# First projection by chunks of tokens with two weight panels side by side, in a decoder step on one core

## The chip, the core and the metric

The kernel runs on one core of a Trainium2 chip. The core has a matrix engine (TensorE; PE in the profile, PEld its weight loads), a vector engine (VectorE, DVE), an engine for scalar functions (ScalarE, ACT), a general engine (GpSimd, POOL) and a queue that issues most transfers (SyncE, SP). The transfers themselves run on 16 DMA engines. Each engine takes its own instructions in order and waits on semaphores for the others. The metric is the device time of one launch in microseconds (us), as the median of several runs; beside it there is one profiled run, whose trace is read here.

## What is computed

One step of a decoder layer with a pooling branch and an attention branch, on 1024 prompt tokens and on 64 sample tokens (8 sequences of 8). All operands are float32. The lines that matter here are the first ones of the layer:

```python
def project(x, ln1, w_in, q_norm, k_norm):
    p = jnp.einsum('btd,de->bte', rms_norm(x, ln1), w_in)
    a, q, k, v, g_a, g_b = jnp.split(p, IN_SPLITS, axis=-1)   # 512 | 768 | 768 | 768 | 1024 | 1024
    ...
# then: a -> causal multi-scale pooling -> linear map -> w_pa; q, k, v -> dilated attention -> w_pb;
# h = x + (sigmoid(g_a) * A + sigmoid(g_b) * B) @ w_o;  y = h + relu(rmsnorm(h) @ w_up)^2 @ w_down
```

`x` has 1024 channels. `rms_norm` divides a token by the root of its mean square and multiplies by `ln1`. The kernel multiplies by `ln1` first, projects, and applies the token's factor afterwards.

## The kernel before

**Layout.** Channels lie on the 128 partitions, tokens along the free axis. 1024 channels are 8 k-tiles (`KD`). The 1088 tokens are taken in three chunks of 384, 384 and 320 columns (`CHUNKS`); the last 64 columns of the third are the sample tokens. The matmul operand `act` holds the tokens ordered by their residue modulo 4, so the split writes them with a stride.

**Two parts of a number.** Each float32 operand is split in two numbers of type fp32r, a high and a low part, and a product is the sum of three passes: high x high, high x low, low x high (`PASSES`). For x, `split_x(c, k)` does it for one k-tile of one chunk: ACT writes the high part (line 312), DVE subtracts it for the low part (line 313). For weights, `split` does the same for 512 columns of a raw panel (ACT line 116, DVE line 117).

**Weight panels.** `w_in` comes in panels of 256 output channels, 8 k-tiles wide. A panel is loaded in four quarters (`fetch`, line 127, 256 KB, two k-tiles each) into three raw buffers used in turn, and split into one of three `places`, also used in turn. The pooling input `a` (512 channels) is the first two panels, so four output tiles of 128 channels; query, key and value panels of head group 2 follow in the next places: the query panel in place 2, the key panel in place 0, the value panel in place 1.

**The first stage.** Twelve matmuls of ones run first (line 360, 24 in the trace, since a plain float32 matmul counts as two). `panel(..., first)` loads and splits panel 0; between its quarters `first(j)` loads the k-tiles 2j and 2j + 1 of chunk 0 (the first two as separate transfers of 192 KB, the others as pairs of 384 KB) and splits them. Then `pool_input(0, wt, c)` runs panel 0 over all three chunks: 48 matmuls a chunk (line 334), pair of k-tiles by pair, in each pair pass by pass, in each pass two output tiles and two k-tiles. `pool_evac` copies the two results from PSUM to `ext` on ACT (line 346; the sample columns line 351). After each chunk's matmuls come the splits of the next chunk. Panel 1 is loaded and split after that, and runs over the three chunks in the same way. There are four PSUM banks for these results, taken in turn.

**Squares.** `square_x(c)` squares the raw x of a chunk in place on ACT (line 304, held back to the matmul before it in the program by `behind_pe`), and POOL adds the four tiles to one (line 306). `x_sums(c)` sums that over the partitions with matmuls against ones (line 369, 12 in the trace) into three PSUM banks `rt`, which DVE reads (line 373). The same three banks serve all chunks. The sums of chunk 0 and 1 stand after panel 1's chunk 0 and 1, those of chunk 2 inside panel 1's chunk 2, when 36 of its 48 matmuls are done. `sample_rows` copies the sample tokens on DVE (line 284). By line 399 the norms of all three chunks are spread for the next stage, whose matmuls (lines 632, 635, 205) begin at once after the projection.

**What sets the order.** PE's order is that of the program (`manual_schedule`). On the other engines, SP's queue included, a planner fixes the order when the program is built: at each step, by its own reckoning of time, it takes from what is ready on the engine the instruction that stands first in the program. That order is then fixed, whatever the chip does; an instruction that waits holds up all behind it on its engine.

Of the kernel before, what the change touches and what calls it, by code (L numbers as in the profile page):

```python
# [15 lines left out]
P = 128  # L16
# [5 lines left out]
CH = 384  # L22
# [15 lines left out]
def decoder_step(ctx, tc, i, o):  # L38
# [10 lines left out]
    def rr(p, shape, dt, name, tag, bufs):  # L49

        n = turn[p, tag] = turn.get((p, tag), -1) + 1
        return p.tile(shape, dt, name=name, tag=f"{tag}.{n % bufs}", bufs=1)
# [38 lines left out]
    def part4(c):  # L91

        return slice(CHUNKS[c][0] // 4, (CHUNKS[c][0] + CHUNKS[c][1]) // 4)
# [12 lines left out]
    def from4(t, sub="p r l -> p l r"):  # L106
        return t.rearrange("p (r l) -> p r l", r=4).rearrange(sub)
# [7 lines left out]
    def split(dst_hi, dst_lo, src):  # L115
        ins = s_.activation(dst_hi, src, AF.Copy)  # L116
        v_.tensor_tensor(dst_lo, src, dst_hi.bitcast(F32), op=ALU.subtract)  # L117
        return ins
# [45 lines left out]
    def panel(src, name, between=None, after=None):  # L164

        n = src.shape[1]
        wt = places[:, place[0] % 3]
        place[0] += 1
        for a in range(0, n, 512):
            raw = fetch(src, name, a)  # L170
            if between is not None:
                between(a // 512)
            ins = split(wt[:, 0, a:a + 512], wt[:, 1, a:a + 512], raw)
            if after is not None:
                behind_pe(ins, after[a // 512])
        throttle.append(ins)
        return wt

    def by_k(wt, kb=KD):
        return wt.rearrange("p s (k n) -> p s k n", k=kb)  # L180
# [69 lines left out]
    def acc_tile(name, tag="acc", bufs=4):  # L250
        return rr(acc_p, [P, 512], F32, name, tag, bufs)
# [17 lines left out]
    def win(name):  # L269
        return rr(xp, [P, LS], F32, name, "win", 2)  # L270
# [10 lines left out]
    def sample_rows():  # L281
        for s in range(2):
            for k in range(KD):
                behind_pe(v_.tensor_copy(smp_t[:, k, s * NS:(s + 1) * NS].rearrange("p (l r) -> p l r", r=4),
                                         act4[s][k][:, :, SEQ // 4:].bitcast(F32).rearrange("p r l -> p l r")))
    xs = {}

    def load_x(c, j):
        c0, n = CHUNKS[c]
        x = rr(xq, [P, 2, CH], F32, name=f"xs{c}_{j}", tag="xs", bufs=12)  # L290
        if c + j == 0:

            dma(x[:, 0, :n], i["xT"][:, 0, c0:c0 + n])
            dma(cols, i["cols"])
        else:
            dma(x[:, :, :n], i["xT"][:, 2 * j:2 * j + 2, c0:c0 + n])
        xs[c, "t", j] = x[:, :, :n]
        for k in range(2):
            xs[c, 2 * j + k] = x[:, k, :n]

    def square_x(c):
        t = [xs[c, "t", j] for j in range(4)]
        for j in (3, 0, 1, 2):
            behind_pe(s_.activation(t[j], t[j], AF.Square))
        for j in range(3):
            g_.tensor_tensor(t[3], t[3], t[j], op=ALU.add)

    def split_x(c, k):
        c0, n = CHUNKS[c]
        hi, lo = (act4[s][k][:, :, part4(c)] for s in range(2))  # L310
        x = xs[c, k].rearrange("p (l r) -> p r l", r=4)
        s_.activation(hi, x, AF.Copy, scale=ln1[:, k:k + 1])  # L312
        v_.scalar_tensor_tensor(lo, x, ln1[:, k:k + 1], hi.bitcast(F32), op0=ALU.mult, op1=ALU.subtract)

    def first(j):
        if j:
            load_x(0, j)
        else:
            dma(xs[0, 1], i["xT"][:, 1, :CH])
        split_x(0, 2 * j)  # L320
        split_x(0, 2 * j + 1)

    L = 15 + SEQ
    LS = L + NB * 23
    exts = {}

    def pool_input(ja, wt, c, middle=None):
        c0, n = CHUNKS[c]
        pts = [acc_tile(f"a{2 * ja + m}_{c}") for m in range(2)]
        for k in range(0, KD, 2):  # L330
            for p, (a, b) in enumerate(PASSES):
                for m in range(2):
                    for kk in (k, k + 1):
                        last_mm[0] = t_.matmul(  # L334
                            pts[m][:, :n], wt[:, a, kk, m * P:(m + 1) * P], act4[b][kk][:, :, part4(c)],
                            start=(p == 0 and kk == 0), stop=(p == 2 and kk == KD - 1))
            if middle and k == 4:
                middle()
        return pts

    def pool_evac(ja, c, pts):
        c0, n = CHUNKS[c]
        for m in range(2):
            ext = exts[2 * ja + m]
            npr = min(n, SEQ - c0)
            s_.copy(ext[:, 15 + c0:15 + c0 + npr].rearrange("p (l r) -> p l r", r=4),
                    from4(pts[m][:, :n])[:, :npr // 4])
            if npr < n:
                new = from4(pts[m][:, :n])[:, npr // 4:].rearrange("p (t q) r -> p q r t", q=2)
                for q in range(2):  # L350
                    s_.copy(ext[:, L:].rearrange("p (b t) -> p b t", b=NB)[:, 4 * q:4 * q + 4, 15:], new[:, q])

    def open_ext(g):
        exts[g] = rr(xp, [P, LS], F32, name=f"ext{g}", tag="ext", bufs=4)
        v_.memset(exts[g][:, :15], 0.0)
# [3 lines left out]
    for _ in range(12):  # L359
        t_.matmul(wu, ones, ones, start=True, stop=True)  # L360
    load_x(0, 0)
    wt = by_k(panel(i["w_in"][0], "a0", first))
    def x_sums(c):
        n = CHUNKS[c][1]
        rt = [rr(ps, [P, 1], F32, name=f"rt{c}_{b}", tag="rt", bufs=3) for b in range(3)]
# [43 lines left out]
            v_.tensor_scalar(xeps[g][:, :8], xg, EPS, None, op0=ALU.mult)  # L409

    v_.memset(rtok[0], 0.0)
    for c in range(3):
        if c < 2:
            for j in range(4):
                load_x(c + 1, j)
        if c == 0:
            open_ext(0)
            open_ext(1)
        pool_evac(0, c, pool_input(0, wt, c))
        if c < 2:  # L420
            for k in range(KD):
                split_x(c + 1, k)
        if c:
            square_x(c - 1)
    square_x(2)
    w1 = by_k(panel(i["w_in"][1], "a1"))
    dma(cst, i["consts"])
    v_.tensor_scalar(wqs, wqc, HD ** -0.5, None, op0=ALU.mult)
    dma(states, i["stateT"].rearrange("g p b t -> p g (b t)"))
    kn = win("kn")[:, :P]  # L430
    for g in range(3):
        dma(kn[2 * g:2 * g + 2], i["qk_norm"][g, 1].rearrange("(j d) -> j d", j=2))
    open_ext(2)
    open_ext(3)
    for c in range(3):
        pool_evac(1, c, pool_input(1, w1, c, (lambda: x_sums(2)) if c == 2 else None))
        if c == 0:
            x_sums(0)
            sample_rows()
        if c == 1:  # L440
            x_sums(1)

            wk = rr(ps, [P, 512], F32, name="wk", tag="wu", bufs=1)[:, :6]
            t_.transpose(wk, kn[:6], ident[:6, :6])
            v_.tensor_tensor(wqk, wqs, wk, op=ALU.mult)
    moving = by_residue()
    next(moving)
    px.close()
# [722 lines left out]
    for g in (2, 1, 0):  # L1171
# [42 lines left out]
        for blks in ((8, 0), (1,), (2,), (3,), (4,), (5,)) + (((6, 7),) if g else ((6,), (7,))):  # L1214
# [12 lines left out]
            for js in (((0, 1), (2,)) if blks[0] in (1, 2, 3, 4, 5) else ((0,), (1,), (2,))):  # L1227
                for b in (blks[::-1] if g < 2 and js == (2,) and 8 in blks else blks):
# [4 lines left out]
                    def middle():  # L1233
                        step()
                        if own:
                            own_step(1)
# [1031 lines left out]
```

## Time and profile before

| what | value |
|---|---|
| time, median of 3 runs | 1401.0 us (1398.73, 1401.0, 1401.69) |
| the profiled run's own time | 1399.09 us |
| its span, first to last instruction | 1397.3 us |
| granted TensorE clock | 1.00 over the whole span |
| busy: PE, DVE, ACT, POOL | 1390.2, 954.0, 756.1, 258.3 us |
| line 334, matmuls of the first projection | 288, from 6.09 us to about 61 us |
| DMA moved | 311.96 MB, mean 223 GB/s |

In the timeline views below, a row gives start and length in us, the engine, the line, the operation, what it writes and reads, the count of merged instructions, and in brackets how long the engine stood idle before the row and what released it. SPq is SP's queue, where a row is the issue of a transfer and not the transfer. A row of the windows gives the stretch, its length, the busy time (and count) of PE, PEld, DVE, ACT and POOL, PE's granted clock, the busy share of the DMA engines and the GB/s that they moved.

### The profile page before, as it was taken

To read this page: it belongs to the slowest core of one execution; us is meant where nothing else is said; L and a number is where in the kernel's file an instruction comes from. 1 tells how busy PE (TensorE), PEld (TensorE's weight loads), DVE (VectorE), ACT (ScalarE), POOL (GpSimd) and SP (SyncE) were. 2 spreads that over 40 slices of the span, in tenths; PEclk is the share of its full clock that TensorE was granted. 3 is DMA by queue.
4 is the path that set the end of the run, shared out by engine and by line. 5 is a ranking of instruction groups with operands and counts; after the bars stand their busy time and mean duration, and the time that the engine had idled before them with its cause. 6 is when DMAs were issued, how large, how long until landed. Compare 5 with 4: busy or idle time off the path is not lost.

```text
span 1397.3 us, 29307 instructions
## 1 busy us (share of the span) xinstructions
PE 1390.2 (99%) x11101; PEld 1341.6 (96%) x11101; DVE 954.0 (68%) x1707; ACT 756.1 (54%) x1787; POOL 258.3 (18%) x362
## 2 busy tenths in 40 slices
PE   9999999999999999999999999999999999999998
PEld 8988987888999999999999999999999999999998
DVE  7788744776876776975559677765665686664565
ACT  8557875787764224554337454554554544444443
POOL 0854356676500000000010000000000000000100
PEclk9999999999999999999999999999999999999999
DMA  6456886755587777956369668765768987777674
GB/s 216 133 166 211 245 246 195 231 139 137 149 248 232 244 220 257 318 194 211 130 199 296 222 217 290 245 204 204 250 202 287 319 274 257 238 239 230 211 256 170
DMA packets 180445, 311.96 MB, mean 223 GB/s; under 512 B 26696, under 2 KB 82318, under 8 KB 178255
## 3 DMA queue, kind: packets, MB, share of 16 engines
q1 hardware_dynamic: 174670, 258.04, 57.8%
q0 software_dynamic: 5632, 52.04, 11.6%
q8 instruction: 87, 1.43, 0.4%
q14 instruction: 56, 0.45, 0.1%
HBM read 239.94 MB, written 122.12 MB: 259 GB/s over the span
## 4 chain that ended last, share of the span: by engine, by line
PE 98%; ACT 0%; DMA 0%; POOL 0%; SPq 0%; issue 0%; DVE 0%; DVEq 0%
PE pz L1330 24%; PE pd L2113 24%; PE pg L1330 12%; PE ph L205 7%; PE pqk L205 6%; PE pab L1330 5%; PE pv L205 5%; PE a L334 3%; PE pk L205 2%; PE pq L205 2%; PE sg0b L702 1%; PE pog0b L735 1%; PE pl L513 1%; PE tpg0b L721 1%; PE sg1b L702 0%; PE tpg1b L721 0%
## 5 line engine op out<-in xcount | busy, mean ns | idle before, releaser
L2113 PE MATMUL pd<-places 128*128 128x272 f32 x2688 | 331.7, 287 | 0.0
L2113 PEld LDWEIGHTS pd<-places 128*128 128x128 f32 x2688 | 331.6, 188 | 0.0
L116 ACT ACTIVATE places<-raw_d 128x544 fp32r<-128x544 f32 (+1 forms) x176 | 110.6, 646 | 159.1 <-DMA raw_d<-z_d 54.8
L2166 POOL DMA_DIRECT2D out_kv_sample_dram<-in_cache_kv_dram x96 | 46.9, 489 | 791.1 <-ACT places L116 582.2
L117 DVE TENSOR_TENSOR places<-raw_d,places 128x544 fp32r<-128x544 f32 (+1 forms) x176 | 122.4, 710 | 90.8 <-ACT places L116 89.0
L1330 PE MATMUL pz<-act,places 128*128 128x280 f32 (+1 forms) x1080 | 139.4, 287 | 0.0
L1330 PEld LDWEIGHTS pz<-act,places 128*128 128x128 f32 x1080 | 135.9, 188 | 0.0
L205 PE MATMUL ph<-act,places 128*128 128x280 f32 (+1 forms) x768 | 96.6, 287 | 0.0
L205 PEld LDWEIGHTS ph<-act,places 128*128 128x128 f32 x768 | 96.0, 188 | 0.1
L1330 PE MATMUL pg<-act,places 128*128 128x264 f32 (+1 forms) x576 | 75.6, 288 | 0.0
L1330 PEld LDWEIGHTS pg<-act,places 128*128 128x128 f32 x576 | 72.6, 188 | 0.6 <-issue 0.3
L1330 PE MATMUL pz<-places,apart 128*128 128x264 f32 (+1 forms) x528 | 67.9, 287 | 0.0
L1330 PEld LDWEIGHTS pz<-places,apart 128*128 128x128 f32 x528 | 66.6, 188 | 0.0
L205 PE MATMUL pqk<-places,act 128*128 128x512 f32 x240 | 60.6, 402 | 0.0
L1330 PE MATMUL pz<-act,apart 128*128 128x264 f32 (+1 forms) x456 | 59.1, 287 | 0.0
L1330 PEld LDWEIGHTS pz<-act,apart 128*128 128x128 f32 x456 | 57.5, 188 | 0.1
L661 POOL TENSOR_TENSOR mr<-ms,mhalf 128x4 f32<-128x4 f32 (+2 forms) x39 | 54.7, 1403 | 2.9 <-POOL ms L660 0.2
L205 PEld LDWEIGHTS pqk<-places,act 128*128 128x128 f32 x240 | 44.8, 192 | 9.6
L886 POOL TENSOR_TENSOR pck<-pck,qs 128x256 f32<-128x256 f32 x64 | 48.6, 791 | 21.1 <-DVE sta L711 12.4
L334 PE MATMUL a<-act,places 128*128 128x384 f32 (+1 forms) x288 | 50.5, 333 | 1.7 <-ACT act L312 1.1
L334 PEld LDWEIGHTS a<-act,places 128*128 128x128 f32 x288 | 47.6, 188 | 3.8 <-ACT act L312 1.9
L1330 PE MATMUL pab<-ab,places 128*128 128x264 f32 (+1 forms) x384 | 50.4, 286 | 0.0
(438 smaller groups left out, 2805.8 us busy)
## 6 DMA issues: line engine op xcount, KB each, us to landing
out_kv_sample_dram<-in_cache_kv_dram POOLq DMA_DIRECT2D x72, 480.0 KB, 5.0
raw_d<-z_d SPq DMA_DIRECT2D x112, 272.0 KB, 4.2
z_d<-t SPq DMA_DIRECT2D x80, 272.0 KB, 3.7
raw_d<-in_w_down_dram SPq DMA_DIRECT2D x80, 256.0 KB, 4.1
raw_u<-in_w_up_dram SPq DMA_DIRECT2D x64, 256.0 KB, 4.3
raw_qkv<-in_w_in_dram SPq DMA_DIRECT2D x36, 256.0 KB, 4.3
own_d<-in_cache_kv_dram POOLq DMA_DIRECT2D x32, 256.0 KB, 3.8
pck<-own_d SPq DMA_DIRECT2D x16, 512.0 KB, 4.8
```

Of the source, the lines that this page charges most:

```text
L116: ins = s_.activation(dst_hi, src, AF.Copy)
L117: v_.tensor_tensor(dst_lo, src, dst_hi.bitcast(F32), op=ALU.subtract)
L205: last_mm[0] = t_.matmul(out, lhs(a, k), rhs(b, k), start=(j == 0), stop=(j == len(terms) - 1))
L334: last_mm[0] = t_.matmul(pts[m][:, :n], wt[:, a, kk, m * P:(m + 1) * P], act4[b][kk][:, :, part4(c)], start=(p == 0 and kk == 0), stop=(p ...
L513: t_.matmul(pl[:, :npr], lin[:, g, :], dp_[:, c0:c0 + npr], start=True, stop=True)
L661: last_norm[0] = g_.tensor_tensor(r[:n, :H], ms[:n, :H], mhalf[:n, :H], op=ALU.pow)
L702: t_.matmul(sc[e][:, hp, j * P:(j + 1) * P], qT[rows, hp, :], kT[rows, 2 + hp, :], start=True, stop=True)
L721: t_.transpose(tp[:, hp * nk + j, :], sms[e][:, hp, j * P:(j + 1) * P], ident)
L886: ins = g_.tensor_tensor(out, *others, op=ALU.mult)
L1330: last_mm[0] = t_.matmul(out[c], lhs(*term), rhs(*term, c), start=(first and n == 0), stop=(n == len(terms) - 1), skip_group_check=not first)
L2113: last_mm[0] = t_.matmul(chain[t][c], A[:, a, t * P:(t + 1) * P], Z[:, b, c], start=(fresh and f == 0 and n == 0), stop=(f == NG - 1 and n ...
L2166: ins = g_.dma_start(d, a)
```

## The change

- `first_panels` takes the place of `panel(..., first)` and of the later load of panel 1: for each pair of k-tiles it loads and splits, in turn, k-tile 2j with panel 0's quarter j, and k-tile 2j + 1 with panel 1's quarter j. Every k-tile of chunk 0 is a transfer of its own, of 192 KB.
- `pool_input(c, then)` runs all four output tiles over a chunk before the next chunk. For chunk 0 the k-tiles 0 to 5 come one by one, each over panel 0's and then panel 1's tiles (for panel 0 from k-tile 1 on with the order of passes `BY_WEIGHT`); the k-tiles 6 and 7 are then done tile by tile. For chunks 1 and 2 each output tile runs to its end, pass by pass over all eight k-tiles, and is copied out at once. `then` says what stands after which tile.
- After chunk 0 stand the splits of chunk 1, the squares of chunk 0, and the loads of the constants and states. After tile 0 of chunk 1 stand the splits of chunk 2, after its tiles 1 and 3 the squares of chunks 1 and 2. In chunk 2 the sums of x for chunks 0, 1 and 2 stand after tile 0 (with the copies of the sample tokens), after tile 1, and after the second of the three passes of tile 3.
- The four `ext` tiles are opened ahead. The number and the shapes of the matmuls stay.

```diff
-    def first(j):
...
+    def first_panels():
+        wts = []
+        for _ in range(2):
+            wts.append(places[:, place[0] % 3])
+            place[0] += 1
+        for j in range(4):
+            if j:
+                t = rr(xq, [P, 2, CH], F32, name=f"xs0_{j}", tag="xs", bufs=12)
+                xs[0, "t", j] = t
+                for k in range(2):
+                    xs[0, 2 * j + k] = t[:, k]
+                dma(t[:, 0], i["xT"][:, 2 * j, :CH])
+            raw = [fetch(i["w_in"][0], "a0", 512 * j)]
+            dma(xs[0, 2 * j + 1], i["xT"][:, 2 * j + 1, :CH])
+            raw.append(fetch(i["w_in"][1], "a1", 512 * j))
+            for ja in range(2):
+                split_x(0, 2 * j + ja)
+                ins = split(*(wts[ja][:, s, 512 * j:512 * j + 512] for s in range(2)), raw[ja])
+        throttle.append(ins)
+        return [by_k(w) for w in wts]
...
-    def pool_input(ja, wt, c, middle=None):
+    BY_WEIGHT = ((0, 0), (1, 0), (0, 1))
+
+    def pool_input(c, then={}):
         c0, n = CHUNKS[c]
-        pts = [acc_tile(f"a{2 * ja + m}_{c}") for m in range(2)]
-        for k in range(0, KD, 2):
+        pts = {}
+
+        def mm(t, a, b, k, start, stop):
+            ja, m = divmod(t, 2)
+            if t not in pts:
+                pts[t] = acc_tile(f"a{t}_{c}")
+            last_mm[0] = t_.matmul(pts[t][:, :n], wt[ja][:, a, k, m * P:(m + 1) * P], act4[b][k][:, :, part4(c)],
+                                   start=start, stop=stop)
+
+        begun = 0 if c else 6
+        if c == 0:
+            for k in (0, 2, 4):
+                for ja in range(2):
+                    for kk in (k, k + 1):
+                        for p, (a, b) in enumerate(PASSES if ja or kk == 0 else BY_WEIGHT):
+                            for m in range(2):
+                                mm(2 * ja + m, a, b, kk, kk == 0 and p == 0, False)
+        for t in range(4):
             for p, (a, b) in enumerate(PASSES):
...
+                for k in range(begun, KD):
+                    mm(t, a, b, k, c > 0 and p + k == 0, p == 2 and k == KD - 1)
+                if p == 1 and (t, 1) in then:
+                    then[t, 1]()
+            pool_evac(t, c, pts[t])
+            if t in then:
+                then[t]()
...
+    THEN = ({}, {0: lambda: split_chunk(2), 1: lambda: square_x(1), 3: lambda: square_x(2)},
+            {0: lambda: (x_sums(0), sample_rows()), 1: lambda: (x_sums(1), key_norms()), (3, 1): lambda: x_sums(2)})
     for c in range(3):
         if c < 2:
             for j in range(4):
                 load_x(c + 1, j)
+        pool_input(c, THEN[c])
         if c == 0:
-            open_ext(0)
-            open_ext(1)
-        pool_evac(0, c, pool_input(0, wt, c))
-        if c < 2:
-            for k in range(KD):
-                split_x(c + 1, k)
-        if c:
-            square_x(c - 1)
-    square_x(2)
-    w1 = by_k(panel(i["w_in"][1], "a1"))
-    dma(cst, i["consts"])
...
+            split_chunk(1)
+            square_x(0)
+        if c == 0:
+            dma(cst, i["consts"])
...
```

More of the change, by code (lines that the diff above doesn't have):

```diff
@@ L313, in split_x @@
         v_.scalar_tensor_tensor(lo, x, ln1[:, k:k + 1], hi.bitcast(F32), op0=ALU.mult, op1=ALU.subtract)
-    def first(j):
[L316 to L321, printed above, removed]
+    def first_panels():
[18 more added lines that the diff above has]
+        return [by_k(w) for w in wts]
     L = 15 + SEQ
@@ L325, in decoder_step @@
     exts = {}
-    def pool_input(ja, wt, c, middle=None):
+    BY_WEIGHT = ((0, 0), (1, 0), (0, 1))
+    def pool_input(c, then={}):
         c0, n = CHUNKS[c]
-        pts = [acc_tile(f"a{2 * ja + m}_{c}") for m in range(2)]
-        for k in range(0, KD, 2):
-            for p, (a, b) in enumerate(PASSES):
[L332 to L339, printed above, removed]
@@ L341, in pool_evac @@
-    def pool_evac(ja, c, pts):
-        c0, n = CHUNKS[c]
[L343 to L351, printed above, removed]
+        pts = {}
@@ new lines, in pool_input, with pool_evac @@
+        for t in range(4):
+            for p, (a, b) in enumerate(PASSES):
+                for k in range(begun, KD):
[5 more added lines that the diff above has]
+                then[t]()
+    def pool_evac(t, c, pt):
+        c0, n = CHUNKS[c]
+        ext = exts[t]
+        npr = min(n, SEQ - c0)
+        s_.copy(ext[:, 15 + c0:15 + c0 + npr].rearrange("p (l r) -> p l r", r=4), from4(pt[:, :n])[:, :npr // 4])
+        if npr < n:
+            new = from4(pt[:, :n])[:, npr // 4:].rearrange("p (t q) r -> p q r t", q=2)
+            for q in range(2):
+                s_.copy(ext[:, L:].rearrange("p (b t) -> p b t", b=NB)[:, 4 * q:4 * q + 4, 15:], new[:, q])
@@ L361, in decoder_step @@
     load_x(0, 0)
-    wt = by_k(panel(i["w_in"][0], "a0", first))
+    wt = first_panels()
     def x_sums(c):
@@ L411, in decoder_step, with key_norms, split_chunk @@
     v_.memset(rtok[0], 0.0)
+    for g in range(4):
+        open_ext(g)
+    def key_norms():
+        wk = rr(ps, [P, 512], F32, name="wk", tag="wu", bufs=1)[:, :6]
+        t_.transpose(wk, kn[:6], ident[:6, :6])
+        v_.tensor_tensor(wqk, wqs, wk, op=ALU.mult)
+    def split_chunk(c):
+        for k in range(KD):
+            split_x(c, k)
+    THEN = ({}, {0: lambda: split_chunk(2), 1: lambda: square_x(1), 3: lambda: square_x(2)},
+            {0: lambda: (x_sums(0), sample_rows()), 1: lambda: (x_sums(1), key_norms()), (3, 1): lambda: x_sums(2)})
     for c in range(3):
@@ L415, in decoder_step @@
                 load_x(c + 1, j)
+        pool_input(c, THEN[c])
         if c == 0:
-            open_ext(0)
-            open_ext(1)
-        pool_evac(0, c, pool_input(0, wt, c))
-        if c < 2:
-            for k in range(KD):
-                split_x(c + 1, k)
-        if c:
-            square_x(c - 1)
-    square_x(2)
-    w1 = by_k(panel(i["w_in"][1], "a1"))
[L427 to L436, printed above, removed]
-        if c == 0:
[L438 to L445, printed above, removed]
+            split_chunk(1)
+            square_x(0)
+        if c == 0:
+            dma(cst, i["consts"])
+            v_.tensor_scalar(wqs, wqc, HD ** -0.5, None, op0=ALU.mult)
+            dma(states, i["stateT"].rearrange("g p b t -> p g (b t)"))
+            kn = win("kn")[:, :P]
+            for g in range(3):
+                dma(kn[2 * g:2 * g + 2], i["qk_norm"][g, 1].rearrange("(j d) -> j d", j=2))
     moving = by_residue()
```

## The prediction

> **What bounds the kernel now.** I read the page first, then who PE waited for, then the first 62 us engine by engine. From the page, the span, the line of PE and the chain that ended last:
>
> ```profile
> span 1397.3 us, 29307 instructions
> PE 1390.2 (99%) x11101; PEld 1341.6 (96%) x11101; DVE 954.0 (68%) x1707; ACT 756.1 (54%) x1787; POOL 258.3 (18%) x362
> ...
> PE 98%; ACT 0%; DMA 0%; POOL 0%; SPq 0%; issue 0%; DVE 0%; DVEq 0%
> ```
>
> TensorE carries the end. An edit that leaves its instructions as they are can win only time in which it stands still, 1397.3 - 1390.2 = 7.1 us in all. Who PE waited for (total, times, longest) puts the named waits into the first stage:
>
> ```profile
> PE a L334 <- ACT act L312: 1.1, 3, 0.4
> ...
> PE a L334 <- ACT places L116: 0.6, 1, 0.6
> ```
>
> A matmul's modelled length hides part of a wait, so I count weight loads instead, one for each matmul of line 334. The timeline of PEld (start, length, count):
>
> ```profile
> 6.09 0.19 PEld L334 LDWEIGHTS a<-act,places 128*128 128x128 f32 x1 [0.78 <-ACT places L116]
> 6.98 0.66 PEld L334 LDWEIGHTS a<-act,places 128*128 128x128 f32 x4 [0.70 <-ACT act L312]
> 7.93 1.19 PEld L334 LDWEIGHTS a<-act,places 128*128 128x128 f32 x7 [0.29 <-DVE act L313]
> 9.68 0.19 PEld L334 LDWEIGHTS a<-act,places 128*128 128x128 f32 x1 [0.56 <-ACT act L312]
> 10.55 0.65 PEld L334 LDWEIGHTS a<-act,places 128*128 128x128 f32 x4 [0.68 <-ACT act L312]
> 11.49 2.05 PEld L334 LDWEIGHTS a<-act,places 128*128 128x128 f32 x12 [0.30 <-DVE act L313]
> 13.80 27.32 PEld L334 LDWEIGHTS a<-act,places 128*128 128x128 f32 x163 [0.26 <-DVE act L313]
> 42.52 8.43 PEld L334 LDWEIGHTS a<-act,places 128*128 128x128 f32 x48
> 52.58 5.29 PEld L334 LDWEIGHTS a<-act,places 128*128 128x128 f32 x36
> ```
>
> Unstalled, 48 matmuls of 384 columns take 8.43 us, 0.176 each; 36 of 320 columns take 5.29, 0.147 each. The 163 from 13.80 on fit this (115 x 0.176 + 48 x 0.147 = 27.3): nothing is lost after 13.80. Before it 29 matmuls took 13.80 - 6.09 = 7.71 us instead of 29 x 0.176 = 5.10. **The start loses 2.6 us**, 0.19% of the time, and that is what there is to win.
>
> ACT and DVE say why. ACT's timeline (line 312 splits x, line 116 weights; then the first evacuation, and two splits of chunk 1 with eight of chunk 2), then DVE's:
>
> ```profile
> 3.41 0.98 ACT L312 ACTIVATE act<-xs,cols 128x384 fp32r<-128x384 f32 x1 [1.17 <-DMA cols<-in_cols_dram]
> 5.41 0.63 ACT L116 ACTIVATE places<-raw_a 128x512 fp32r<-128x512 f32 x1 [1.02 <-DMA raw_a<-in_w_in_dram]
> 5.95 0.98 ACT L312 ACTIVATE act<-xs,cols 128x384 fp32r<-128x384 f32 x1
> 7.24 0.63 ACT L116 ACTIVATE places<-raw_a 128x512 fp32r<-128x512 f32 x1 [0.31 <-DMA raw_a<-in_w_in_dram]
> 8.65 1.85 ACT L312 ACTIVATE act<-xs,cols 128x384 fp32r<-128x384 f32 x2 [0.77 <-DMA xs<-in_xT_dram]
> 10.40 0.62 ACT L116 ACTIVATE places<-raw_a 128x512 fp32r<-128x512 f32 x1
> 10.92 3.63 ACT L312 ACTIVATE act<-xs,cols 128x384 fp32r<-128x384 f32 x4
> 14.45 0.62 ACT L116 ACTIVATE places<-raw_a 128x512 fp32r<-128x512 f32 x1
> ...
> 20.26 0.83 ACT L346 COPY ext<-a 128x384 f32<-128x384 f32 x2
> 20.99 7.96 ACT L312 ACTIVATE act<-xs,cols 128x384 fp32r<-128x384 f32 x10
> ```
>
> ```profile
> 6.07 0.69 DVE L117 TENSOR_TENSOR places<-raw_a,places 128x512 fp32r<-128x512 f32 x1 [0.74 <-ACT places L116]
> 6.96 0.92 DVE L313 SCALAR_TENSOR_TENSOR act<-xs,cols,act 128x384 fp32r<-128x384 f32 x1 [0.20 <-ACT act L312]
> ```
>
> On ACT a split of x comes every 0.88 us (10.92 to 14.45 for 4), one of weights every 0.52 (10.40 to 10.92). A pair of k-tiles costs ACT 2 x 0.88 + 0.52 = 2.3 us and gives PE only 12 matmuls, 2.1 us. PE is faster than its feed.
>
> **The change, part by part.** *Both panels at once.* Matmuls stay 288, their forms too. A pair of k-tiles now costs ACT 2 x (0.88 + 0.52) = 2.8 us and gives PE 24 matmuls, 4.2 us: the feed gets ahead. I walk the first pair. x0, first quarter of panel 0, x1 and a quarter of 256 KB are issued in the order of before, so the first matmul stays at 6.09. Six matmuls of k-tile 0 run to 7.15; their weights' low part is there at 6.07 + 0.69 = 6.76, needed at 6.79. k-tile 1 has its high part at 5.95 + 0.98 = 6.93. Weights by weights, its low part is wanted last, at 7.85, and is there at 6.96 + 0.92 = 7.88. Panel 1's quarter is split where panel 0's second was, 7.24 to 7.87, wanted at 8.3. Loss: some 0.1 us. Pair 1 is wanted from 10.4 on. x2, 192 KB instead of the 384 KB that landed at 8.65, lands some 0.5 us sooner and is split on ACT from 8.15 to 9.1, its weights to 9.7; on DVE their low part is done at 10.75 and wanted two matmuls later, at 10.74: just in time. k-tile 3 and panel 1 are 0.5 to 1.3 us early by the same steps, later pairs more. **Gain 2.5 us**, bounds 2.0 (a late landing in pair 1) and 2.6 (all of it).
>
> *Smaller and more loads of x.* Three more issues at 0.45 us of SP's queue, in time in which SP stands waiting for a raw buffer (4.55 to 6.79, below); bytes are the same. Chunk 0 now wants 8 x 192 KB + 8 x 256 KB = 3.67 MB. The windows (last figures: DMA share, GB/s) say what arrives:
>
> ```profile
> 0.00:5.00 5.00, 3.94 (x21) 3.94 (x22) 1.09 (x9) 2.47 (x3) 0.20 (x4) 1.00 0.48 122
> 5.00:10.00 5.00, 3.72 (x18) 2.53 (x16) 2.98 (x5) 3.50 (x5) 0.00 (x0) 1.00 1.01 342
> 10.00:15.00 5.00, 4.58 (x24) 3.88 (x23) 5.00 (x7) 5.00 (x8) 0.00 (x0) 1.00 1.06 399
> ```
>
> 0.61 + 1.71 = 2.32 MB by 10 us, the rest 1.35 / 0.4 = 3.4 us later: 13.4. PE wants the last pair at 6.2 + 72 x 0.176 = 18.9. Cost nothing, unless a quarter is held up on SP (third rival).
>
> *Chunk 1, tile by tile.* Chunk 0 ends at 6.1 + 0.1 + 96 x 0.176 = 23.1. Then tile 0 asks for the high parts of all eight k-tiles within 8 x 0.176 = 1.4 us, where pairs had 2.1 us each. The eighth is wanted at 24.3. ACT: if chunk 0's sixteen splits run to some 16.7 (pair 0 to 7.8, pairs 1 to 3 with 2.8 each, a quarter waiting 0.5 us), chunk 1's eight take 7.0, to 23.7; each evacuation put among them adds 0.37 (20.26: 0.83 for two). With one or two of four: 24.1 to 24.4. **Cost 0.4 us**, bounds 0 and 1.5 (four evacuations among them). Low parts are wanted 1.4 us later and follow ACT by 1 us.
>
> *Squares sooner.* Chunk 0's and 1's squares move beside the splits of chunk 2. ACT from 23.7 on: four evacuations 1.5, squares of chunk 0 at 0.77 (below) 3.1, eight splits of 320 columns 6.2 ((20.99: 7.96 - 2 x 0.88) / 8 = 0.78 each): 34.5; chunk 2 is wanted at 23.5 + 96 x 0.176 = 40.4. Cover 5.9 us, cost nothing. The adds on POOL move too, and the sums of x move together: the sums for chunk 1 follow those for chunk 0 by one tile of chunk 2, 24 x 0.147 = 3.5 us, where 8.4 us lay between (42.52: 48 matmuls). They reuse its three banks, which DVE must have read. Before, from ACT, POOL, DVE and PE:
>
> ```profile
> 30.63 3.05 ACT L304 ACTIVATE xs<-xs 128x768 f32<-128x768 f32 x4
> ```
>
> ```profile
> 32.30 16.72 POOL L306 TENSOR_TENSOR xs<-xs,xs 128x768 f32<-128x768 f32 x8 [31.85 <-ACT xs L304]
> ```
>
> ```profile
> 34.24 4.64 DVE L117 TENSOR_TENSOR places<-raw_a,places 128x512 fp32r<-128x512 f32 x2 [2.55 <-ACT places L116]
> ...
> 47.52 2.07 DVE L284 CAST smp_t<-act 128x64 fp32r<-128x64 f32 x5
> ...
> 50.88 0.15 DVE L373 TENSOR_SCALAR stats<-rt 128x1 f32<-128x1 f32 x1
> ```
>
> ```profile
> 51.11 1.39 PE L369 MATMUL rt<-ones,xs 128*128 128x1 f32 x12
> ...
> 66.80 0.57 PE L632 MATMUL pk<-places,smp_t 128*128 128x256 f32 x1
> ```
>
> The last read of the first sums ended at 51.03, the next sums began at 51.11: in time, with nothing over. DVE was late because POOL's adds (16.72 / 8 = 2.09 us each) stretched its subtractions from 0.69 to 4.64 / 2 = 2.3 us. Now chunk 2's squares wait for chunk 1's end (40.4), its three adds run from about 43 to 50, and the reads (sums of chunk 0 over at 45.3) are wanted at 48.9. **Cost 0.2 us**, bounds 0 (reads of 0.15 us slip in between) and 1.3 (all wait for POOL).
>
> [...]
>
> [...]
>
> *Place of panel 0.* It comes free after tile 1 of chunk 2, near 49 instead of 33 (13.80 + 67 x 0.176 + 48 x 0.147), so the key panel's four splits (ACT 0.52, DVE 0.69 each, 3 us) end by 53; its first matmul was at 66.8, and would be near 65. Hidden by 12 us.
>
> **Sum:** -2.5 + 0.4 + 0.2 = **-1.9 us**. The profiled run took 1399.09 (span 1397.3 and 1.8 around it) and would take 1397.2; the median shown lies 1.9 above it, at 1401.0, and becomes **1399.1**.
>
> **The rivals.** (1) *All of it comes*, no new wait: -2.5 or a little more, 1398.5. For it: my costs are edges of tenths. (2) *Chunk 1 takes it back*: the eight high parts come 1.5 to 2.5 us late, the start's wait moves to 23 us; net -1.0 to 0, 1400.5. For it: in the rows above ACT has no idle time after 8.65, so it had nothing to spare. (3) *POOL's adds keep the three banks*, as above, and chunk 2's low parts come late behind them too: 1.3 to 2 us given back, 1400.5. (4) *Slower: loads of x overtake the raw quarters.* Three raw buffers turn round, so from the fourth quarter on each issue waits for a split; the planner may then put the loads of chunks 1 and 2, which wait for nothing, in front. SP before:
>
> ```profile
> 4.55 0.47 SPq L296 DMA_DIRECT2D xs<-in_xT_dram  x1
> 6.79 0.34 SPq L127 DMA_DIRECT2D raw_a<-in_w_in_dram  x1
> 7.18 5.16 SPq L296 DMA_DIRECT2D xs<-in_xT_dram  x8
> ...
> 14.95 0.33 SPq L427 DMA_DIRECT2D cst<-in_consts_dram  x1
> ```
>
> The fourth quarter kept its turn (6.79), against the rival; the constants, behind all of panel 1 in the program, went ahead of its later quarters, for it. Panel 0's third quarter would land near 11 and is wanted, split, at 14.7. Each 384 KB ahead of it costs 1 us: three are free, from the sixth on the gain is gone; all eight (2.88 MB, 7.2 us) bring it at 19.6, split at 20.3: 5.7 us of waiting, net +3.2, 1404.2.
>
> **How the numbers follow.** Forecast (-1.9) 0.50; all of it 0.16; chunk 1 takes it back 0.16; POOL 0.10; overtaking 0.08. The three runs shown spread over 3 us, and 0.2% (2.8 us) is about what a measurement can tell from no change. No summed case wins 2.8; the scatter puts about half of "all of it" and a third of the forecast there: faster 0.25. Slower: overtaking, in part, and scatter of rivals 2 and 3: 0.08. Same 0.67. The range goes from the fastest run shown less 2.5 (1396.2) to rivals 2 and 3 with 1 us of scatter (1401.6); it leaves out overtaking.
>
> **What would show it.** Right: PE's first matmul near 6.1, chunk 0's 96 matmuls over by 23.2 without waits over 0.2 us; a wait of PE for line 312 near 24; the sums of x one tile apart with under 1 us idle. Wrong: waits of line 334 for raw_a after 14, loads of chunk 1 on SP ahead of raw_a; idle of PE between 40 and 60; or time that moved behind 62 us, where I expect only a shift.

## The result, and the profile after

The changed kernel takes **1405.32 us** (median of 7 runs, 1402.45 to 1409.43); the kernel before, on the same chip, 1399.37 (7 runs, 1398.51 to 1401.69). The ratio is 1.0039, 95% interval 1.0023 to 1.0055: slower by 0.4%, some 6 us. The prediction was 1399.1, in a range of 1396.2 to 1401.6, with 0.08 for slower. It was wrong in size and in sign, and the time lies outside the range. What happened is the fourth rival, and a fall of the clock that no part of the prediction had.

The profiled run is the longest of the seven, 1409.43 with a span of 1407.7. PE's work stays at 11101 matmuls, and its busy time is longer, which pauses alone would not make it:

```profile
span 1407.7 us, 29315 instructions
PE 1396.0 (99%) x11101; PEld 1345.8 (96%) x11101; DVE 956.4 (68%) x1707; ACT 756.6 (54%) x1787; POOL 260.7 (19%) x362
```

PEld's timeline of after (the projection is now line 350, the sums line 397; the last row is the first weight load of the next stage), and the one row of PE's waits that names line 350:

```profile
6.21 8.85 PEld L350 LDWEIGHTS a<-act,places 128*128 128x128 f32 x50
15.36 1.69 PEld L350 LDWEIGHTS a<-act,places 128*128 128x128 f32 x10 [0.31 <-DVE places L117]
18.21 0.65 PEld L350 LDWEIGHTS a<-act,places 128*128 128x128 f32 x4 [1.16 <-ACT places L116]
19.23 1.36 PEld L350 LDWEIGHTS a<-act,places 128*128 128x128 f32 x8 [0.38 <-DVE places L117]
23.99 27.70 PEld L350 LDWEIGHTS a<-act,places 128*128 128x128 f32 x144 [3.39 <-ACT places L116]
...
56.50 1.45 PEld L397 LDWEIGHTS rt<-ones,xs 128*128 128x128 f32 x12
...
66.42 0.19 PEld L655 LDWEIGHTS pq<-places,smp_t 128*128 128x128 f32 x1
```

```profile
PE a L350 <- ACT places L116: 3.9, 2, 3.1
```

The first 50 matmuls run without a gap: the start's loss of 2.6 us is gone. Then PE stands still for split weights, four times, in all 23.99 - 6.21 - 72 x 0.176 = 5.1 us. And the 144 matmuls from 23.99 on (120 of 384 columns, 24 of 320) should take 24.65 us by the rates of before and take 27.70: 3.05 more, with no wait between them. The windows say what that is (stretch, length, busy time of PE, PEld, DVE, ACT, POOL, then PE's clock):

```profile
20.60:23.16 2.56, 0.32 (x2) 0.00 (x0) 2.56 (x4) 2.56 (x4) 0.00 (x0) 1.00 1.00 319
23.16:26.57 3.41, 2.58 (x8) 2.58 (x9) 2.48 (x6) 1.03 (x3) 0.00 (x0) 0.50 0.87 301
26.57:29.99 3.42, 3.42 (x13) 3.42 (x12) 1.16 (x2) 2.51 (x5) 0.00 (x0) 0.50 0.38 104
29.99:33.40 3.41, 3.41 (x21) 3.41 (x20) 3.07 (x5) 3.41 (x6) 0.00 (x0) 1.00 0.07 26
```

During the pause the granted clock falls to a half, and it stays there for 6.83 us. The next stage starts at 66.42; in the kernel before it started here:

```profile
60.88 0.19 PEld L632 LDWEIGHTS pq<-places,smp_t 128*128 128x128 f32 x1
```

So **+5.5 us at the end of the projection = -2.6 (start) + 5.1 (pauses) + 3.0 (half clock)**. Not all of the 3.0 is the clock's: in e4 below, whose clock never falls, the 120 matmuls from chunk 1 on take 20.79 us where the rates give 20.4, so some 0.4 us comes with taking chunk 1 tile by tile, and the half clock cost about 2.7. The medians differ by 5.95 us, close to this sum, but the sum is read from one profiled run. The other six have no trace, and their mean clock on record (0.998 to 1.000, against 0.997 in the profiled one) leaves open whether each stood at half clock as long. The 4 us by which the profiled run is longer than the median lie scattered behind the projection; the repeat below (e6_again) has nearly the same first 66 us and a span of 1403.6.

Why the weights come late stands in the order of two queues. SP's timeline of after (line 127 raw quarters, here the last three; 296 pairs of chunk 1; 463 and 465 constants and states), then ACT's (line 116 weights, 312 splits of x, 375 copies):

```profile
9.50 0.43 SPq L296 DMA_DIRECT2D xs<-in_xT_dram  x1
10.08 0.36 SPq L127 DMA_DIRECT2D raw_a<-in_w_in_dram  x1
10.48 2.16 SPq L296 DMA_DIRECT2D xs<-in_xT_dram  x3
12.74 0.81 SPq L127 DMA_DIRECT2D raw_a<-in_w_in_dram  x1
13.59 0.51 SPq L463 DMA_DIRECT2D cst<-in_consts_dram  x1
14.75 0.38 SPq L465 DMA_DIRECT2D states<-in_stateT_dram  x1
15.78 0.33 SPq L127 DMA_DIRECT2D raw_a<-in_w_in_dram  x1
```

```profile
17.50 0.66 ACT L116 ACTIVATE places<-raw_a 128x512 fp32r<-128x512 f32 x1
18.02 5.40 ACT L312 ACTIVATE act<-xs,cols 128x384 fp32r<-128x384 f32 x6
23.28 0.65 ACT L116 ACTIVATE places<-raw_a 128x512 fp32r<-128x512 f32 x1
26.31 0.48 ACT L375 COPY ext<-a 128x384 f32<-128x384 f32 x1 [2.38 <-PE a L350]
26.69 0.63 ACT L116 ACTIVATE places<-raw_a 128x512 fp32r<-128x512 f32 x1
```

All four loads of chunk 1 were issued ahead of the last two quarters, one of them ahead of the last three, and the constants and the states ahead of the last one; and on ACT six splits of chunk 1, wanted after chunk 0, stand ahead of the two quarters that chunk 0 still needs. ACT works without a pause from 18.02 to 23.9, while PE waits from 20.59 to 23.99.

### The profile page after: what moved, and what is told of

Its sections match the earlier page's. It is cut to its first block, busy times and chain, and to the rows that moved or that the text cites. A ratio compares the mean times of both kernels' runs of the same rounds, so it can differ in the third digit from the quotient of the medians.

```text
span 1407.7 us, 29315 instructions
## 1 busy us (share of the span) xinstructions
PE 1396.0 (99%) x11101; PEld 1345.8 (96%) x11101; DVE 956.4 (68%) x1707; ACT 756.6 (54%) x1787; POOL 260.7 (19%) x362
## 4 chain that ended last, share of the span: by engine, by line
PE 71%; DMA 1%; ACT 1%; DVE 0%; SPq 0%; issue 0%; DVEq 0%; ACTq 0%
PE pd L2136 23%; PE pz L1353 22%; PE pg L1353 12%; PE ph L205 7%; PE pab L1353 5%; DMA u<-u_d 0%; DMA raw_d<-in_w_down_dram 0%; PE pog0b L758 0%; PE sg0b L725 0%; PE tpg0b L744 0%; ACT places L116 0%; PE pk L205 0%; PE pv L205 0%; SPq L1847 0%; PE pq L205 0%
## 5 line engine op out<-in xcount | busy, mean ns | idle before, releaser
L350 PEld LDWEIGHTS a<-act,places 128*128 128x128 f32 x288 | 50.6, 197 | 5.5 <-ACT places L116 4.5
```

The costliest lines, as they stand in the source:

```text
L350: last_mm[0] = t_.matmul(pts[t][:, :n], wt[ja][:, a, k, m * P:(m + 1) * P], act4[b][k][:, :, part4(c)], start=start, stop=stop)
```

## The experiments

Three questions: is it the order of the loads and splits; what does the clock cost by itself; does the forecast's sum hold once both are gone? All kernels were timed against the kernel before on their chip (medians 1399.91, 1399.82 and 1400.53 for e1 to e4, e5 to e8, e9 and e10). The fourth column is the start of the next stage in the profiled run (60.88 before, 66.42 after), the fifth how long the clock stood at a half before 74 us (for e2 and e3 the clock was read up to 40 us; behind that their 40 matmuls between the second and third sums took 5.86 and 5.87 us, as in e4; between 74 and 1396 us the clock was 1.00 in before and in after).

| kernel | median, us (runs) | ratio, 95% interval | next stage | half clock |
|---|---|---|---|---|
| e1_keep_order | 1405.92 (5) | 1.0046, 1.0033 to 1.0058 | 65.71 | 6.83 |
| e2_splits_only | 1405.59 (5) | 1.0047, 1.0034 to 1.0061 | 66.65 | 3.41 |
| e3_fill | 1402.87 (9) | 1.0027, 1.0018 to 1.0037 | 64.14 | 0 |
| e4_buffers | 1399.21 (11) | 0.9996, 0.9987 to 1.0005 | 59.84 | 0 |
| e5_evac_first | 1400.57 (12) | 1.0002, 0.9994 to 1.0011 | 61.53 | 3.41 |
| e6_again | 1405.40 (5) | 1.0039, 1.0027 to 1.0051 | 66.51 | 6.83 |
| e7_before_buffers | 1406.37 (5) | 1.0051, 1.0039 to 1.0063 | 67.17 | 3.41 |
| e8_squares_late | 1408.82 (5) | 1.0059, 1.0046 to 1.0072 | 68.91 | 10.24 |
| e9_sums_later | 1399.05 (11) | 0.9989, 0.9980 to 0.9998 | 58.94 | 0 |
| e10_fill_less | 1406.59 (5) | 1.0038, 1.0024 to 1.0052 | 65.71 | 3.41 |

### The order held by hand, with three raw buffers (e1, e2)

`keep` adds an edge that fixes only the planner's order. e1 holds the later loads (x of chunks 1 and 2, constants, states, norms) behind the last quarter's load, and the splits of chunks 1 and 2 behind its split; e2 has only the edge on the splits, the second below.

```diff
+            if c:
+                keep(ins, last_fetch[0])
...
+        if c:
+            keep(ins, throttle[0])
...
-            dma(cst, i["consts"])
+            keep(dma(cst, i["consts"]), last_fetch[0])
```

> The changed kernel with its order held: on SP's queue all loads of chunks 1 and 2, of the constants and of the states stand behind the last raw quarter, and on ACT the splits of chunk 1 behind the split of the last quarter. Theory A (the quarters of the last two pairs were overtaken, PE stood still near 20 to 24 us, and its clock then dropped to half for some 7 us): no wait of PE over 1 us before 24 us, clock 1.00 throughout, 1396 to 1400 us, 0.1 to 0.2% below the kernel before. Theory B (chunk 1 tile by tile, or the squares and POOL's adds beside chunk 2, cost it): 1403 to 1407 us as the changed kernel.

> Only ACT's order is held: the splits of chunk 1 and 2 behind the split of the last quarter; SP's queue stays as the planner made it, so four loads of chunk 1 and the constants still go ahead of the last quarters. If ACT's order alone is the cause: as e1, 1396 to 1400 us. If the late quarters on SP's queue are part of it: the last quarter is split near 20 to 24 us, chunk 1's splits follow it and end near 28 to 31, and PE waits 3 to 6 us at the start of chunk 1: 1403 to 1408 us.

Neither is faster than after. e1 missed the first theory's time; 1405.92 lies in the second theory's range, but for another reason than that theory names: chunk 1's x came late. e2 came out by its second theory: the late quarters on SP's queue are part of the cause. In e1 (PEld, SP, then ACT; line 359 is the projection, 128 the raw quarters, 301 the pairs of x, 319 the splits of x):

```profile
6.11 1.74 PEld L359 LDWEIGHTS a<-act,places 128*128 128x128 f32 x10
8.16 15.05 PEld L359 LDWEIGHTS a<-act,places 128*128 128x128 f32 x86 [0.31 <-DVE act L322]
28.37 22.61 PEld L359 LDWEIGHTS a<-act,places 128*128 128x128 f32 x120 [5.17 <-ACT ext L384]
```

```profile
10.16 5.02 SPq L128 DMA_DIRECT2D raw_a<-in_w_in_dram  x3
15.22 1.96 SPq L301 DMA_DIRECT2D xs<-in_xT_dram  x4
```

```profile
20.89 7.07 ACT L319 ACTIVATE act<-xs,cols 128x384 fp32r<-128x384 f32 x8 [1.86 <-DMA xs<-in_xT_dram]
```

Chunk 0 now runs through, its 96 matmuls over at 23.2 as the prediction had it. But the last three quarters took SP until 15.2, since each waits for one of three buffers, and chunk 1's x stands behind them: ACT could begin its splits only at 20.89, and PE pauses 5.17 us at chunk 1 instead. (What ends the pause is the first copy out of PSUM, which stands on ACT behind the eight splits, over at 27.96.) In e2, SP's order is that of after, and its ACT shows that the seventh quarter had not landed:

```profile
20.07 0.63 ACT L116 ACTIVATE places<-raw_a 128x512 fp32r<-128x512 f32 x1 [3.00 <-DMA raw_a<-in_w_in_dram]
```

PE pauses 1.50 and 1.41 us for the last two quarters, and then for chunk 1's splits one by one, five times 0.7 us and once 0.2, 6.6 us in all. So holding the order does not put it right: **in the three orders tried with three raw buffers (after, e1, e2) either the last quarters or chunk 1 is late, or both**, by 5.1 to 6.6 us. Other orders, such as loads of chunk 1 put singly between the last quarters, were not tried.

### More buffers (e4)

Quarters 4 to 7 of the eight are loaded into the slots that chunk 2's x takes later, so that of all quarters only the last one waits for a buffer, which the first one's split sets free.

```diff
+    def quarter(ja, j):
+        n = 2 * j + ja
+        if n < 3 or n > 6:
+            return fetch(i["w_in"][ja], f"a{ja}", 512 * j)
+        raw = xq.tile([P, 2, CH], F32, name=f"rawx{n}", tag=f"xs.{5 + n}", bufs=1).rearrange("p s n -> p (s n)")[:, :512]
+        dma(raw, i["w_in"][ja][:, 512 * j:512 * j + 512])
+        return raw
...
-            raw = [fetch(i["w_in"][0], "a0", 512 * j)]
+            raw = [quarter(0, j)]
...
```

> No order held, but four of the eight quarters go to buffers that chunk 2's x takes later, so that only the last quarter's load waits for a split and nothing has cause to overtake. Theory A: quarters in the program's order on SP and ACT, PE's waits before 24 us under 0.5 us, clock 1.00, 1396 to 1399 us; a rest of 0 to 1.5 us of waiting at the start of chunk 1 is possible. Theory B: 1403 to 1407 us.

The rows of e4: SP (line 127 is the last quarter, 296 chunk 1), PEld, ACT.

```profile
10.36 0.33 SPq L127 DMA_DIRECT2D raw_a<-in_w_in_dram  x1
10.79 2.15 SPq L296 DMA_DIRECT2D xs<-in_xT_dram  x4
```

```profile
6.29 16.90 PEld L358 LDWEIGHTS a<-act,places 128*128 128x128 f32 x96 [0.82 <-ACT places L116]
24.32 20.79 PEld L358 LDWEIGHTS a<-act,places 128*128 128x128 f32 x120 [1.14 <-ACT ext L383]
```

```profile
16.70 7.21 ACT L312 ACTIVATE act<-xs,cols 128x384 fp32r<-128x384 f32 x8
23.82 1.19 ACT L383 COPY ext<-a 128x384 f32<-128x384 f32 x3
```

The last quarter is issued at 10.36 instead of 15.78, and ahead of chunk 1. All 96 matmuls of chunk 0 run in 16.90 us, 0.176 each, the clock never falls, and 6 us of loss are gone: 0.9996 against after's 1.0039, intervals apart. The median, 1399.21, lies just above the first theory's 1399. No order was held by hand here, so the cause is shown: too few raw buffers, by way of the order that the planner made of them. One pause is left, 1.14 us at chunk 1. It is not a late split, as the forecast had it, but the first copy out of PSUM, which waits on ACT behind all eight splits; chunk 1 needs its bank.

### The clock by itself (e3, e10)

The changed kernel, with matmuls of ones on ones into the warm-up's bank while PE waits: nine in e3, three in e10.

```diff
+        if c == 0:
+            for _ in range(9):
+                t_.matmul(wu, ones, ones, start=True, stop=True)
         for t in range(4):
```

> The changed kernel with 9 more matmuls of ones on ones (18 in the trace, some 3.2 us) ahead of k-tiles 6 and 7 of chunk 0, whose result nobody reads: PE has work while it waits for the quarters. Theory A: the quarters come as late as before (the last one somewhat sooner, since the planner puts its split before the first evacuation), but the clock stays at 1.00 instead of 0.5 for 7 us: 3 to 3.5 us less than the changed kernel, 1401 to 1403 us, and runs closer together. If the clock did not follow from PE's idling: 1404 to 1407 us, with a clock under 1 near 24 us.

> The changed kernel with three matmuls of ones on ones (about 0.7 us) ahead of k-tiles 6 and 7 of chunk 0, a third of e3's nine. The longest pause of TensorE is then about 2.6 us instead of 3.4. Theory A (the half clock needs a pause that fills most of a 3.4 us stretch): the clock stays at 1.00 or falls for one stretch of 3.4 us only, and the time is 1402.5 to 1404. Theory B (the clock answers the idle share of a fixed stretch, and the 2.6 us stand beside another 1.3 us pause): it still falls to a half for 3.4 to 6.8 us from about 23 us, and the time is 1404 to 1405.5. In both the stall itself stays, so not below 1402.

e3's PEld shows the weights as late as in after (24.08 for 23.99), with most of the pause filled:

```profile
20.59 2.15 PEld L363 LDWEIGHTS wu<-ones 128*128 128x128 f32 x18
24.08 0.66 PEld L350 LDWEIGHTS a<-act,places 128*128 128x128 f32 x4 [1.33 <-ACT places L116]
```

The clock stays at 1.00, and the next stage begins 66.42 - 64.14 = 2.3 us sooner: useless work made the projection end sooner in the profiled run, so the fall of the clock is a cost of its own, beside the pause. The median, 1402.87, is in the first theory's range and 2.5 us below after's, but the intervals of the two ratios overlap (1.0018 to 1.0037, 1.0023 to 1.0055), so for the whole kernel the gain is likely and not shown. With three matmuls the clock still falls, for one stretch of 3.41 us instead of two, which both theories allowed, so e10 does not decide between them; its median, 1406.59, lies above both ranges (the next stage starts 0.7 us sooner than in after, and the ratio is not told apart from after's).

### What stands behind the pause (e5, e9)

e5 is e4 with the first copy ahead of the splits of k-tiles 5 to 7 of chunk 1 on ACT. e9 is e5 with the sums of chunk 1 one output tile later (the last two lines below).

```diff
+        if c == 1 and k >= 5:
+            keep(ins, copied[0, 0])
...
-            {0: lambda: (x_sums(0), sample_rows()), 1: lambda: (x_sums(1), key_norms()), (3, 1): lambda: x_sums(2)})
+            {0: lambda: (x_sums(0), sample_rows()), 1: lambda: key_norms(), 2: lambda: x_sums(1), (3, 1): lambda: x_sums(2)})
```

> e4 with one order held on ACT: the copy of chunk 0's first output tile stands ahead of the splits of k-tiles 5, 6 and 7 of chunk 1, so that its PSUM bank is free when chunk 1 starts. In e4 PE waited 0.8 us (1.14 us on weight loads) for that copy, which stood behind all eight splits. If that bank is the whole rest: a wait under 0.4 us at 23 to 25 us, 0.7 to 1.1 us below e4, 1398 to 1398.6 us, 0.1% below the kernel before. If ACT's sum is the limit there (eight splits and one copy end later than chunk 0): the wait stays at 0.5 to 1 us with the split of k-tile 7 as its cause, 1398.6 to 1399.3 us.

> The kernel of e5 with one line's place changed: the sums of x of chunk 1 (twelve one-column matmuls) stand after tile 2 of chunk 2 instead of after tile 1. In e5 TensorE waited there 0.38 and 0.15 us for GpSimd's adds, and the granted clock fell to a half from about 51.9 us for 3.4 us, in the profiled execution; e5's runs spread from 1397.6 to 1402.8. Theory A (that thin stretch, and the half clock that it sets off, is all that stood between e5 and the forecast's mechanics): no wait for GpSimd, clock 1.00 in every stretch to 74 us, the projections of q start at 59.2 to 59.9 (before: 60.88), and 1397.3 to 1398.3, a ratio of 0.998 to 0.999. Theory B (the gain of taking both panels at once is given back later in the kernel, whatever the clock does): the projection ends as early, but 1399 to 1400.5.

In e5 the pause at chunk 1 shrank from 1.14 to 0.56 us, as meant, and the kernel was no faster than e4 (1.0002 against 0.9996, intervals overlapping; the median, 1400.57, lies above both ranges). Its profiled run, 1402.63 us and so one of the slower ones, shows what happened there, in PEld, DVE and windows (line 412 is the sums of x, 416 DVE's reading of them, 288 the copies of the sample tokens):

```profile
45.89 3.52 PEld L365 LDWEIGHTS a<-act,places 128*128 128x128 f32 x24
49.79 0.52 PEld L412 LDWEIGHTS rt<-ones,xs 128*128 128x128 f32 x4 [0.38 <-POOL xs L310]
50.46 1.07 PEld L412 LDWEIGHTS rt<-ones,xs 128*128 128x128 f32 x8 [0.15 <-DVE stats L416]
```

```profile
44.86 4.75 DVE L288 CAST smp_t<-act 128x64 fp32r<-128x64 f32 x5 [0.32 <-PE a L365]
49.53 0.14 DVE L416 TENSOR_SCALAR stats<-rt 128x1 f32<-128x1 f32 x1
```

```profile
48.30:51.71 3.41, 3.19 (x24) 2.81 (x22) 3.41 (x20) 1.58 (x5) 2.93 (x4) 1.00 0.00 0
51.71:55.12 3.41, 3.41 (x14) 3.41 (x14) 1.91 (x11) 0.21 (x1) 3.41 (x3) 0.50 0.56 171
```

PE is ready for the second sums at 49.41, half a microsecond sooner than in e4 (49.92), and DVE has not yet read the banks of the first ones: its reads begin at 49.53, behind copies of which five took 4.75 us beside POOL's adds, and the next five, from 49.60 on, behind the add's end, 0.68 (in e4 the first read was at 48.82). That is the third rival, 0.53 us. The profile puts the first wait down to an add of POOL; but the add that ended at 49.41 is one of chunk 2's, which these sums don't read, so DVE's read is the likelier releaser. Those twelve matmuls have one column each, so with the wait PE does little for some 2 us, and the clock falls for 3.41 us. That costs another 1.5: the 40 matmuls behind the sums take 7.40 us, 5.87 in e4. In e9, with the sums one tile later, PEld has:

```profile
6.34 37.77 PEld L365 LDWEIGHTS a<-act,places 128*128 128x128 f32 x216 [1.05 <-ACT places L116]
...
52.79 1.45 PEld L412 LDWEIGHTS rt<-ones,xs 128*128 128x128 f32 x12
...
58.94 0.19 PEld L670 LDWEIGHTS pq<-places,smp_t 128*128 128x128 f32 x1
```

No wait for POOL, 216 matmuls on end, clock 1.00 in every stretch, and the next stage at 58.94: **1.94 us sooner than before, where the forecast's sum was 1.9**. The median is 1399.05 against 1400.53, ratio 0.9989 (0.9980 to 0.9998), faster than both kernels, if only just: -0.3 to -2.8 us. It falls above the first theory's 1397.3 to 1398.3 as a number, since the kernel before also ran 0.7 us longer on that occasion than beside e5; as a ratio it is inside. It also lies in the second theory's 1399 to 1400.5, by which the gain is given back later, and the two profiled spans differ by only 0.4 us (1396.9 and 1397.3), less than single runs scatter. So the gain is shown up to the end of the projection; whether part of it is lost again later stays open.

### Repeat, buffers in the kernel before, and squares late (e6, e7, e8)

e6 is after, unchanged. e7 is the kernel before with panel 0's last quarter in slot 8 of x. e8 is e5 with the squares of all chunks after chunk 1.

```diff
+    aside = {("a0", 1536): 8}
...
-            raw = fetch(src, name, a)
+            raw = raw_quarter(src, name, a)
```

```diff
-    THEN = ({}, {0: lambda: split_chunk(2), 1: lambda: square_x(1), 3: lambda: square_x(2)},
+    THEN = ({}, {0: lambda: split_chunk(2), 3: lambda: (square_x(0), square_x(1), square_x(2))},
...
             split_chunk(1)
-            square_x(0)
```

> The changed kernel once more, nothing edited, on the chip of these runs. Theory A: the quarters again late, PE idle for some 3 us between 20 and 24 us, half clock for one stretch of about 7 us behind it, 1402 to 1407 us; the small waits of the first profile behind 300 us (0.7 us for natt, 0.8 and 0.2 us near 760 us) are scatter and come elsewhere or not at all. If those later waits belong to the change: the same waits at the same places.

> The kernel before with a fourth buffer for panel 0's last quarter, so that none of the first panel's loads waits for a split. If buffers alone gave e4 its time (and two panels at once nothing): the start's loss of 2.6 us shrinks here too, by 1 us or more, 1398 to 1399 us. If the start of the kernel before is held by ACT, which splits 2.3 us for 2.1 us of matmuls: its loss stays at 2 to 2.6 us, 1399.5 to 1400.5 us.

> e5 with the squares of chunks 0 and 1 later, behind chunk 1 together with those of chunk 2; the sums stay where the change has them. If the squares' earlier place is needed for the sums' place: POOL's nine adds (2.1 us each) run from about 41 to 60 us, PE waits 2 to 6 us at the sums of chunk 0 and again later, its clock halves for a stretch, 1403 to 1412 us. If squares sooner make no difference: as e5.

e6 gave after's ratio again, 1.0039, with its largest pause (3.38 us) and its half clock (6.83 us). The small waits of after's profile behind 300 us did not come again; one of them (0.7 us for `natt`) stands in e5's profile too, so they look like scatter and not like the change.

e7's time missed both ranges: one moved quarter cost 6.5 us. ACT and PEld of e7 (line 322 splits x, 344 is the projection):

```profile
27.46 1.66 ACT L116 ACTIVATE places<-raw_a 128x512 fp32r<-128x512 f32 x3
29.02 1.63 ACT L322 ACTIVATE act<-xs,cols 128x320 fp32r<-128x320 f32 x2
```

```profile
16.23 9.65 PEld L344 LDWEIGHTS a<-act,places 128*128 128x128 f32 x55 [0.25 <-DVE act L323]
29.93 0.19 PEld L344 LDWEIGHTS a<-act,places 128*128 128x128 f32 x1 [4.05 <-ACT act L322]
```

After 96 matmuls, chunks 0 and 1, PE wants the first two k-tiles of chunk 2. Their load now waits for slot 8, and the planner has put their splits last, behind three quarters of panel 1: a pause of 4.05 us, and 3.41 us of half clock. It is the same kind of fault as in after, made by a smaller edit. What e7 was made for, its trace still answers: up to 16.23 its 41 matmuls took 9.82 us from the first one at 6.41 instead of 41 x 0.176 = 7.2. The start's loss stays at 2.6 us, as the second theory said, so the buffer for the last quarter was not what held it.

e8 gave 1408.82, within its expected range. Its POOL began its adds at 43.00, PE paused 6.14 us at the first sums, and the clock stood at a half from 48.5 to 58.7:

```profile
50.31 2.63 PEld L412 LDWEIGHTS rt<-ones,xs 128*128 128x128 f32 x12 [6.14 <-POOL xs L310]
```

So the early squares are needed where the change puts the sums: without them the sums would be what is late.

## Why the prediction was wrong

- **The start: right.** First matmul at 6.21 (said: near 6.1), 50 matmuls without a gap, and chunk 0 in e4 in 16.90 us for 96 x 0.176. The loss of 2.6 us went. ACT's sum was right too: in e4 chunk 1's splits begin at 16.70 (said: 16.7) and end at 23.9 (23.7).
- **"Smaller and more loads of x ... Cost nothing, unless a quarter is held up on SP": this step failed.** (It names the third rival there; the fourth is meant.) I counted bytes, and put the last pair at 13.4, wanted at 18.9; in after the last two quarters were split on ACT from 23.28 and 26.69, and PE waited 5.1 us where the sum had nothing. I did not walk the last four quarters through three buffers and two queues, though each waits for the split of the quarter three places earlier, while chunk 1's loads and splits wait for nothing. They stood in front, on SP and on ACT. e4 shows that the buffers decide it.
- **The fourth rival had the right fault and, by luck, nearly the right price.** It said 5.7 us of waiting, measured 5.1. But its own terms don't give 5.7: 11 + 7.2 is 18.2 and not 19.6, so with the split the quarter would be there at 18.9, 4.2 us late, net +1.7. And it had all eight loads ahead of panel 0's third quarter. In after that quarter was 0.3 us late at most (on ACT from 13.66, wanted at 14.7); half of the eight loads, and the splits on ACT, which it did not have, held up the last three. Its chance, 0.08, was too small: the ground was that one quarter had kept its turn in the kernel before, while the constants, in the same fence, had not.
- **The clock was no term of any sum.** The rows of before show 1.00 throughout, so there was nothing to read the price from, but a rival with a pause of 5.7 us left its consequence out, some 2.7 us in after. That the rival's +3.2 and these 2.7 add up to 5.9, where the medians differ by 5.95, is luck, since +3.2 is not what its terms give.
- **Chunk 1 tile by tile:** with its cover restored the pause was 1.14 us (e4), inside the bounds of 0 to 1.5, above the 0.4 chosen. The cause differed: I had counted copies put among the splits as a cost; it was the copy put behind them. With the copy ahead it is 0 to 0.56 (e9, e5). Beside the pause, the matmuls from chunk 1 on take 0.4 us more than their rates give, in e4 and in e9 alike.
- **Squares and sums:** nothing in after, since PE was late. In e5 0.53 us by the third rival's way, with a half clock behind it that was not foreseen. What the third rival counts for chunk 2's low parts was an estimate: no row of before shows them beside the adds. In after two of them took 2.15 us each beside POOL's adds, four 0.77 each without them (line 313 on DVE, 37.80 and 29.52); PE did not wait for them.
- **Panel 0's place:** no wait for it in any of these runs, as said.
- **The sum of -1.9** is close to e9's -1.94, but not term by term. In e9 neither of the sum's two costs shows, no pause at chunk 1 and none at the sums, so by its own terms it would win 2.5. In their place the first matmul comes 0.25 us later than before (6.34 and 6.09), and the 216 matmuls take 37.77 us where the rates give 37.3. So the agreement is partly luck. What e9 shows is that two panels at once end the projection some 2 us sooner, once the buffers and the two orders are changed as well; the change as made does not.

What stays open: by what reckoning the planner chose that order (only the order itself was seen); why e5's runs reach from 1397.63 to 1402.82 (the fall of the clock was seen in its profiled run alone, and the mean clocks on record, 0.998 to 1.000, do not sort the others: 1401.53 had 1.000); why matmuls taken tile by tile are a little slower; and the 4 us that after's profiled run lost behind 66 us.

## What to carry to other kernels

When loads that wait for a buffer and loads that wait for nothing share a queue whose order a planner fixes, count the buffers before the bytes: walk the last user of each buffer through the load queue and through the engine that frees it. Price a pause of TensorE at its length plus, where the clock falls with it, a little under half of the work time at low clock (here 2.7 us for 6.0, and 1.5 for 3.4); where a pause can't be removed, matmuls on idle data can be cheaper than standing still, by 2.3 us up to the next stage in e3's profiled run. And when a stall goes, look at what it hid: here two smaller ones, 1.14 us in e4, and in e5 0.53 us with 1.5 us of half clock, which add up to more than the 2.6 us that the start gave.

## What the runs showed of the hardware

The half clock came only in whole multiples of 3.41 us: 3.41 in e2, e5, e7 and e10, 6.83 in after, e6 and e1, 10.24 in e8. Pauses of 1.1 to 1.5 us between dense matmuls (e2, e3, e4) didn't set it off; in e2 it fell behind a stretch without a pause over 0.7 us, but with four matmuls only (PEld busy for 0.74 of 3.41 us). In e10's stretch before the fall PEld was busy 0.76 of 3.41 us; the stretch at a half that followed was nearly full, and the clock came back:

```profile
21.33:24.74 3.41, 0.95 (x8) 0.76 (x7) 3.41 (x5) 3.04 (x4) 0.00 (x0) 1.00 0.90 272
24.74:28.15 3.41, 3.41 (x12) 3.26 (x11) 1.96 (x6) 1.01 (x2) 0.00 (x0) 0.50 0.75 265
28.15:31.56 3.41, 3.41 (x21) 3.41 (x21) 1.99 (x4) 3.19 (x5) 0.00 (x0) 1.00 0.29 77
```

In after the first stretch at a half had 0.83 us of the pause left in it (PEld 2.58), and the clock stayed down for a second. That reads as if the activity of each stretch set the clock of the next, but no run decides it. The clock also fell where PE did not stand still for most of a stretch: in e5 it fell after one in which PEld was busy for 2.81 us, 1.59 of them with loads for matmuls of one column. e8 reads the same way: there the clock stayed down for a third stretch behind one in which PEld was busy throughout (3.41 us), 1.04 us of it with loads for matmuls of one column.
